# Layer 1 of a hybrid encoder: four pairs of projection tiles as quads of seven block products

## The chip, the cores and the metric

The kernel runs on one core of a Trainium2 chip. The metric is the device time of one execution in microseconds (us). Five engines with queues of their own work side by side: TensorE (PE, with its weight loads shown as PEld), VectorE (DVE), ScalarE (ACT), GpSimd (POOL) and SyncE (SP). On POOL and SP this kernel only issues transfers.

## The reference, cut to what matters

Two layers over 1024 positions of width 1024. Each layer begins with a norm and one wide projection:

```
hn = rmsnorm(h, norm1_g[layer])
proj = hn @ w_in[layer]                     # 1024 x 3328
u, q, k, v = proj[..., :512], proj[..., 512:1024], proj[..., 1024:1152], proj[..., 1152:1280]
gate_a, gate_b = sigmoid(proj[..., 1280:2304]), sigmoid(proj[..., 2304:])
y_a = s5_branch(u, ...)                     # two-way state-space scan, 32 groups, gelu, GLU
y_b = windowed_gqa(q, k, v, ...)            # 8 heads, blocks of 128 positions, window 128
merged = gate_a * (y_a @ w_branch_a) + gate_b * (y_b @ w_branch_b)
h = h + merged @ w_out;   h = h + swiglu_ffn(rmsnorm(h, norm2_g[layer]))
```

## The kernel before, in words

Activations lie transposed: 128 channels on the partitions, 1024 positions in two halves of 512 (h is 0 or 1). The 3328 columns of `w_in` are 26 tiles of 128: four of u, four of q (q0 to q3), one of k, one of v, eight of gate a (`ga`) and eight of gate b (`gb`). A half tile is one output of 128x512. Every fp32 operand is split into a high and a low part (`split`, `parts`), and a product of two operands takes three matmuls, so a half tile of a projection (`chain`, L175 to L177) is 8 blocks of 128 channels x 3 = 24 matmuls of 512 columns. Splitting the weights of a tile costs one cast on ACT (`whi`) and one subtraction on DVE (`wlo`), each 128x1024.

Work is a list of items, emitted in order (`emit`); the framework's scheduler then fixes the order of every engine's instructions when the program is compiled. Items that carry weights (`Granule`) also start loads of later weights. At most three plain weight tiles are split at a time. Activations lie in 86 slots of 128x512, and PSUM has 8 banks.

In layer 1 the items come in this order:

- The norm of both halves (`norm_parts`: `n0`, `n1`). The first half is normed while layer 0's last products run, the second between the first projections. PE works meanwhile on k, v and q0, first with half 0.
- q0, q1 and two half tiles of u.
- Attention (`attention_items`): 18 steps. Step i takes `round(per * (i + 1))` half tiles in all from the filler list (two more near the end), then computes the scores of unit i, the values of unit i - 2 and the transposes of unit i - 1. A unit is a key head group and a block of 128 queries. Here `per` is 1 and the list is two half tiles of u, then q2 and q3 (needed for the second key head), the rest of u and all gates: 42 half tiles. From step 12 on each step also starts one state scan (`s5_states`, q = 0 to 5).
- The S5 loop (`s5_items`): 9 iterations, again with filler, `per` 2. Iteration i has the output of state pair i (`s5_output`, PSUM tile `s5y`), and in i = 1 to 5 the states q = 2i + 4 and 2i + 5 (PSUM tile `s5x`, then on DVE L948 to L964, then four copies on ACT into `s5sg`, L968). The output of pair i needs the states 2i and 2i + 1, which the two iterations before have started. Between output and store lie a square on ACT, `s5w` on DVE (L997), a tanh on ACT (L998) and `s5g` on DVE (L1005).
- Four half tiles of filler around the loads of z, then the GLU, both branch products and `w_out`.

Layer 0 has the same attention and the same S5 loop, with 0.6 and 2.2 half tiles for `per`, and later in its loop half tiles of the branch product (`br`, 12 matmuls each) as filler.

The FFN already has a form that multiplies a pair of weight tiles against both halves of the positions as 2x2 blocks in the manner of Strassen and Winograd: seven block products in place of eight. A block product is 4 blocks of channels x 3 = 12 matmuls (`piece`, L186 to L188). `sums` forms sixteen combinations of the normed activations on DVE, `sum_pairs` splits them (`T`, 16 pairs, names `tt0` to `tt3`), `quad_part` forms the combinations of weights.

Of the kernel before, what the change touches and what calls it, by code (L numbers as in the profile page):

```python
# [8 lines left out]
F32 = mybir.dt.float32  # L9
# [4 lines left out]
ADD, SUB, MUL = ALU.add, ALU.subtract, ALU.mult  # L14
# [7 lines left out]
HC = 512  # L22
# [9 lines left out]
M_U, M_Q, M_K, M_V, M_GA, M_GB = 0, 4, 8, 9, 10, 18  # L32
# [63 lines left out]
class Trunk:  # L96
# [579 lines left out]
    def w_in(self, l, m):  # L676
        return Granule(self.t["w_in"][l, m].rearrange("p k c -> p (k c)"), DM)

    apart = None
# [185 lines left out]
    def attention_items(self, l, keys, q23, fill, per, tail):  # L865


        stage = {}
        fill = (list(fill[:2]) if l else []) + q23 + list(fill[2 if l else 0:])

        def scores(u):
            stage[u] = self.att_scores(l, u // 8, u % 8)

        def scale(u):
            self.att_scale(l, u // 8, *stage[u])

        def transpose(u):
            ex, k0, k1, _ = stage[u]
            stage[u] = (self.att_transpose(ex, k0, k1), k0, k1)

        def values(u):
            self.att_values(u // 8, u % 8, *stage.pop(u))

        taken = 0
        for i in range(18):
            want = min(len(fill), round(per * (i + 1)) + max(0, i - 15))
            self.add(fill[taken:want])
            taken = max(taken, want)
# [12 lines left out]
            self.add(tail.get(i, []))  # L901
            if i in (5, 7):
                self.add([keys[(i - 1) // 2]])
        return fill[taken:]

# [211 lines left out]
        return early, split, out  # L1117


    def w_out_items(self, l):  # L1120
        nc, V = self.nc, self.nc.vector
        self.h2 = {}
# [2 lines left out]
        src = self.t["xt"] if l == 0 else self.hs  # L1125
# [43 lines left out]
    def ffn_items(self, l, fill, head):  # L1169

        nc, V = self.nc, self.nc.vector
# [4 lines left out]
        early = quads < 4  # L1176
        ys = {} if early else None
# [48 lines left out]
        n0, n1 = (self.norm_parts(h, "rf", 2 * l + 1, lambda m, h=h: self.h2[m, h], lambda: self.hn2, ys) for h in range(2))  # L1226
        main = []
        blocks = []
        T = [[None] * 4 for _ in range(4)]

        def sums(j):

            at = ((j, 0), (j, 1), (j + 4, 0), (j + 4, 1))
            if early:
                y11, y12, y21, y22 = (ys.pop(a) for a in at)
            else:
                y11, y12, y21, y22 = (self.A("y") for _ in at)
                for y, (m, h) in zip((y11, y12, y21, y22), at):
                    hi, lo = self.hn2[h][m]
                    V.tensor_tensor(y, hi.bitcast(F32), lo.bitcast(F32), ADD)  # L1240
            V.tensor_tensor(y11, y12, y11, SUB)
            V.tensor_tensor(y12, y22, y12, SUB)
            V.tensor_tensor(y22, y22, y11, SUB)
            V.tensor_tensor(y21, y21, y22, SUB)
            for k, y in enumerate((y11, y22, y12, y21)):
                T[k][j] = (y, None)

        def sum_pairs(j, k):
            T[k][j] = self.split(T[k][j][0], f"tt{k}")

        def quad_items(f):

            q = Quad(self.t["w_gate"][l, f].rearrange("p k c -> p (k c)"), self.t["w_up"][l, f].rearrange("p k c -> p (k c)"))
            b = {}

            def product(bank, g, off, xs, start):
                def run():
                    if start:
                        b[bank] = self.PS(f"q{bank}")
                    self.piece(b[bank], g, off, xs(), start)  # L1260
                return (run, g)

            B = lambda h, a: lambda: self.hn2[h][a:a + 4]
            p = [product("x", q.a, 0, B(0, 0), True), product("y", q.b, HC, lambda: T[1], True),
                 product("v", q.b, 0, lambda: T[0], True), product("x", q.a, HC, B(0, 4), False),
                 product("y", q.c, 0, lambda: T[2], False), product("w", q.d, 0, lambda: T[3], True),
                 product("v", q.e, 0, B(1, 4), False)]

            def first():
                b["p1"] = self.A("qp")  # L1270
# [44 lines left out]
        made = {f: quad_items(f) for f in range(quads, NFF)}  # L1315
        orders = {}
        for gi, (f0, n) in enumerate(groups):
            for f in range(f0, f0 + n):
                if f in made:
                    p, e = made[f]  # L1320
# [29 lines left out]
            if f0 + n == quads:  # L1350
# [6 lines left out]
                w = 4 if early else 12  # L1357
# [4 lines left out]
        if fill:  # L1362
            a = len(head) + 12
            b = fill_end
# [4 lines left out]
    def build(self):  # L1369
        nc, V = self.nc, self.nc.vector  # L1370
# [30 lines left out]
        for l in range(DEPTH):  # L1401
# [23 lines left out]
            n0, n1 = (self.norm_parts(h, "ra", 2 * l, lambda m, h=h, src=src: src(m, h), lambda: self.hn) for h in range(2))  # L1425
            v1, v2 = self.halves(vc[0])
            loads, states = self.s5_head(l)
            tail_items = {11: pairs[:1] if l == 0 else []}
# [23 lines left out]
                self.add(pairs[1:])  # L1452
            else:

                k1, k2 = self.halves(kc[0])
# [174 lines left out]
```

## Time and profile before

| what | value |
|---|---|
| median of three runs | 2649.34 us (2649.23 to 2649.55) |
| the profiled execution | 2650.72 us, its span 2648.9 us |
| PE busy / DVE busy / ACT busy | 98% / 63% / 40% of the span |
| mean granted clock of TensorE | 0.993 |

The span runs from the first to the last instruction of the profiled execution; 1.8 us of its time lie outside. Busy shares are of the span; a matmul of 512 columns shows about 390 ns although the next one starts earlier, so a busy PE is read by the distance of starts.

### The profile page before, as it was taken

How to read it: one execution, taken by the hardware profiler on the slowest of the kernel's cores; microseconds unless marked ns; L12 is line 12 of the kernel's file. 1: busy time of each engine (PE TensorE's matmuls, PEld its weight loads, DVE VectorE, ACT ScalarE, POOL GpSimd, SP SyncE). 2: the span in 40 equal slices, each digit the busy share in tenths (PEclk: the TensorE clock that was granted, in tenths of full speed). 3: DMA queues.
4: the chain of work that ended last, by engine and by line, in shares of the span. 5: the costliest groups of instructions: out<-in, count | busy, mean ns of one | idle time of the engine just before them, and what ended most of it. 6: DMA issues, size and time to landing. Idle time of an engine off the chain costs nothing.

```text
span 2648.9 us, 35135 instructions
## 1 busy us (share of the span) xinstructions
PE 2590.7 (98%) x12878; PEld 2108.2 (80%) x12878; DVE 1659.1 (63%) x3333; ACT 1058.1 (40%) x2037; POOL 359.5 (14%) x524
## 2 busy tenths in 40 slices
PE   8999999999999999999999999999999999999997
PEld 6786677887788888888877778888878888888886
DVE  8985878575986745544673576646376545654556
ACT  5335743422443433333344553343235433333332
POOL 0141001000142220121010001100002220122010
PEclk9999999999999999999999999999999999999998
DMA  3453345354283652564342235434315652455253
GB/s 138 134 186 114 126 136 180 118 188 143 60 203 106 124 108 62 110 126 96 78 170 76 72 128 184 147 121 166 128 64 113 132 124 61 92 121 114 60 108 135
DMA packets 157438, 321.36 MB, mean 121 GB/s; under 512 B 20768, under 2 KB 55840, under 8 KB 157264
## 3 DMA queue, kind: packets, MB, share of 16 engines
q1 hardware_dynamic: 106192, 201.68, 23.1%
q0 software_dynamic: 51072, 117.43, 20.3%
q8 instruction: 101, 1.65, 0.3%
q14 instruction: 73, 0.60, 0.1%
HBM read 196.37 MB, written 122.63 MB: 120 GB/s over the span
## 4 chain that ended last, share of the span: by engine, by line
PE 89%; DVE 7%; DMA 2%; ACT 2%; issue 1%; SPq 0%; DVEq 0%; ACTq 0%
PE pj L175 6%; PE pj L176 6%; PE pj L177 6%; PE dn L175 6%; PE dn L176 6%; PE dn L177 6%; PE qy L186 2%; PE qx L186 2%; PE qv L186 2%; PE qv L188 2%; PE qy L188 2%; PE qx L188 2%; PE qv L187 2%; PE qx L187 2%; PE qy L187 2%; PE wo L175 2%
## 5 line engine op out<-in xcount | busy, mean ns | idle before, releaser
L164 DVE TENSOR_TENSOR wlo<-raw,whi 128x1024 fp32r<-128x1024 f32 (+3 forms) x210 | 186.3, 887 | 265.6 <-ACT whi L163 254.6
L163 ACT CAST whi<-raw 128x1024 fp32r<-128x1024 f32 (+3 forms) x210 | 163.8, 780 | 365.7 <-PE pj L176 118.0
L175 PE MATMUL pj<-rah,whi 128*128 128x512 f32 x768 | 306.1, 399 | 1.0 <-ACT rah L112 1.0
L176 PE MATMUL pj<-ral,whi 128*128 128x512 f32 x768 | 300.7, 392 | 1.3 <-DVE ral L113 1.3
L177 PE MATMUL pj<-rah,wlo 128*128 128x512 f32 x768 | 300.2, 391 | 0.0
L1208 POOL DMA_DIRECT2D hs<-dx x208 | 179.1, 869 | 845.0 <-ACT dx L1207 731.0
L175 PEld LDWEIGHTS pj<-rah,whi 128*128 128x128 f32 x768 | 145.0, 189 | 35.2 <-issue 3.3
L176 PEld LDWEIGHTS pj<-ral,whi 128*128 128x128 f32 x768 | 144.8, 189 | 31.4 <-DVE ral L113 3.2
L177 PEld LDWEIGHTS pj<-rah,wlo 128*128 128x128 f32 x768 | 144.8, 188 | 30.8
L1207 ACT COPY dx<-dn 128x512 f32<-128x512 f32 x208 | 121.2, 584 | 76.3 <-PE dn L177 75.6
L796 DVE CUSTOM_DVE_ANT_0 x<-s,bias,nsink 128x384 f32<-128x384 f32 (+1 forms) x128 | 67.6, 578 | 67.9 <-PE s L790 67.3
L186 PE MATMUL qx<-rfh,whi 128*128 128x512 f32 x280 | 108.9, 389 | 0.0
L187 PE MATMUL qx<-rfl,whi 128*128 128x512 f32 x280 | 108.9, 389 | 0.0
L188 PE MATMUL qx<-rfh,wlo 128*128 128x512 f32 x280 | 108.9, 389 | 0.0
L968 ACT COPY s5sg<-s5s 64x256 f32<-64x256 f32 x128 | 51.7, 404 | 132.8 <-DVE s5s L963 125.1
L175 PE MATMUL wo<-mgh,whi 128*128 128x512 f32 x256 | 100.0, 391 | 0.0
L177 PE MATMUL wo<-mgh,wlo 128*128 128x512 f32 x256 | 99.6, 389 | 0.0
L176 PE MATMUL wo<-mgl,whi 128*128 128x512 f32 x256 | 99.6, 389 | 0.0
L112 ACT CAST ffah<-ts 128x512 fp32r<-128x512 f32 x35 | 21.7, 621 | 191.2 <-DVE ts L1290 191.2
L175 PE MATMUL dn<-ffbh,whi 128*128 128x512 f32 x232 | 91.3, 394 | 0.0
L176 PE MATMUL dn<-ffbl,whi 128*128 128x512 f32 x232 | 90.6, 390 | 0.0
L176 PE MATMUL dn<-ffal,whi 128*128 128x512 f32 x232 | 90.4, 390 | 0.0
(430 smaller groups left out, 6695.7 us busy)
## 6 DMA issues: line engine op xcount, KB each, us to landing
hs<-dx POOLq DMA_DIRECT2D x208, 256.0 KB, 6.2
raw<-in_w_in SPq DMA_DIRECT2D x52, 512.0 KB
raw<-in_w_gate SPq DMA_DIRECT2D x44, 512.0 KB
raw<-in_w_up SPq DMA_DIRECT2D x44, 512.0 KB
raw<-in_w_down SPq DMA_DIRECT2D x96, 192.0 KB
g<-th POOLq DMA_DIRECT2D x64, 256.0 KB, 2.8
thr<-g SPq DMA_DIRECT2D x64, 256.0 KB
hs<-h POOLq DMA_DIRECT2D x48, 256.0 KB, 2.3
```

Source lines behind the costliest of these rows:

```text
L163: nc.scalar.copy(g.hi[:, :n], g.raw[:, :n])
L164: nc.vector.tensor_tensor(g.lo[:, :n], g.raw[:, :n], g.hi[:, :n].bitcast(F32), SUB)
L175: mm(ps, lhsT=wh, rhs=xh, start=k == 0, stop=False)
L176: mm(ps, lhsT=wh, rhs=xl, start=False, stop=False)
L177: mm(ps, lhsT=wl, rhs=xh, start=False, stop=k == n - 1)
L186: mm(ps, lhsT=wh, rhs=xh, start=start and k == 0, stop=False)
L187: mm(ps, lhsT=wh, rhs=xl, start=False, stop=False)
L188: mm(ps, lhsT=wl, rhs=xh, start=False, stop=k == len(xs) - 1)
L796: V.tensor_tensor_reduce(out=x[:, :n], in0=ps[:, :n], in1=self.bias[hd][:, bo:bo + n], op0=ADD, op1=ALU.min, scale=-1.0, scalar=self.nsink ...
L968: nc.scalar.copy(SG[64 * r:64 * r + 64, g * 256:(g + 1) * 256].rearrange("p (d n) -> p d n", d=2), Sv[64 * g:64 * g + 64, :, r])
L1207: nc.scalar.copy(t, ps)
L1208: nc.gpsimd.dma_start(self.hs[m, h], t, accum_op=ADD)
```

## The change

In layer 1 the eight tiles u0 to u3, k with v, and q0 with q1 become four quads. `tile_u`, `tile_kv` and `tile_q` are called with `grab` set, which collects their tile numbers and their closing functions; `linear_quads` then builds the seven products of each pair, sums the four results on DVE (five additions) and one copy on ACT, and hands each half tile to the closing function. The sixteen sums and their splits are formed once and serve all four quads. Three tiles of gate b, as plain products, take the place of k, v and q0 at the start of the layer. All four key tiles are made before attention. The filler list of attention and S5 loop is now q2, q3 and thirteen gate tiles (30 half tiles), and `per` falls from 1 to 0.9 and from 2 to 1. In numbers, with Python's rounding: steps 4 and 15 of attention get no filler, the other sixteen steps as many as before; in the S5 loop each iteration gets one half tile in place of two, and three in place of four are left behind the loop.

```diff
+        if self.grab is not None:
+            self.grab.append((m, done))
+            return []
...
-        fill = (list(fill[:2]) if l else []) + q23 + list(fill[2 if l else 0:])
+        fill = q23 + list(fill)
...
+    def quad_products(self, src1, src2, pairs, T):
+        q = Quad(*(s.rearrange("p k c -> p (k c)") for s in (src1, src2)))
...
+        return [product("x", q.a, 0, B(0, 0), True), product("y", q.b, HC, lambda: T[1], True),
+                product("v", q.b, 0, lambda: T[0], True), product("x", q.a, HC, B(0, 4), False),
+                product("y", q.c, 0, lambda: T[2], False), product("w", q.d, 0, lambda: T[3], True),
+                product("v", q.e, 0, B(1, 4), False)], b
...
+    def linear_quads(self, l, made, T):
...
+            def first(b=b):
+                b["p1"] = self.A("qp")
+                nc.scalar.copy(b["p1"], b["x"])
+            def second(b=b):
+                b["u2"] = self.A("qu")
+                V.tensor_tensor(b["u2"], b["p1"], b["y"], ADD)
+            def out11(b=b, done=done1):
+                done(0, b["x"])
+            def sum22(b=b):
+                V.tensor_tensor(b["p1"], b["p1"], b["y"], ADD)
+                b["c22"] = self.A("qc")
+                V.tensor_tensor(b["c22"], b["p1"], b["v"], ADD)
+            def out2(b=b, done=done2):
+                V.tensor_tensor(b["p1"], b["p1"], b["w"], ADD)
+                done(0, b["p1"])
+                done(1, b["c22"])
+            def out12(b=b, done=done1):
+                V.tensor_tensor(b["u2"], b["u2"], b["v"], ADD)
+                done(1, b["u2"])
...
+                us = self.linear_quads(l, [lambda i=i: self.tile_u(l, i) for i in range(4)], T)
+                kvq = self.linear_quads(l, [lambda: self.tile_kv(l, M_K, kn), lambda: self.tile_kv(l, M_V, vn),
+                                            lambda: self.tile_q(l, 0), lambda: self.tile_q(l, 1)], T)
+                a, c = (self.halves(x) for x in (gb[0], gb[2]))
...
-                         [k1, n1[0], k2, v1, n1[1], n1[2], v2, n1[3], n1[4], n1[5], qc[0], ke[0], ve[0], qe[0], kc[1], ke[1],
-                          vc[1], ve[1]] + keys[:2] + [qc[1], qe[1], vals, bias0] + q1 + us[:2])
-                left = self.attention_items(l, keys, q23, us[2:] + gb + ga, 1, tail_items)
+                         [a[0], n1[0], a[1], c[0], n1[1], n1[2], c[1], n1[3], n1[4], n1[5], gb[4], *s[:2], gb[1], *s[2:], *sp[1],
+                          gb[3], *sp[0], gb[5], *sp[2], *sp[3]] + us + kvq[:15] + keys + kvq[15:17] + [vals] + kvq[17:] + [bias0])
+                left = self.attention_items(l, [None] * 4, q23, gb[6:] + ga, 0.9, tail_items)
...
-                left = self.s5_items(l, left, 2)
+                left = self.s5_items(l, left, 1)
```

`sums` and `sum_pairs` move unchanged from `ffn_items` into functions of their own, and `gb[2m]`, `gb[2m + 1]` are the two half tiles of gate tile m.

## Rows read from the trace of the kernel before

**Rows 1.** The page: busy time, then its share in 40 slices.

```profile
PE 2590.7 (98%) x12878; PEld 2108.2 (80%) x12878; DVE 1659.1 (63%) x3333; ACT 1058.1 (40%) x2037; POOL 359.5 (14%) x524
PE   8999999999999999999999999999999999999997
```

**Rows 2.** Windows by stage, layer 1: stretch, length, busy PE, PEld, DVE, ACT, POOL.

```profile
1424.00:1539.00 115.00, 115.00 (x679) 85.75 (x678) 60.75 (x218) 64.97 (x175) 4.87 (x9) 1.00 0.25 83
1539.00:1602.80 63.80, 61.95 (x389) 46.69 (x388) 45.37 (x123) 30.16 (x72) 3.28 (x7) 1.00 0.30 100
...
1632.60:1696.90 64.30, 64.30 (x417) 53.58 (x416) 52.86 (x110) 25.77 (x53) 14.40 (x24) 1.00 0.54 180
...
1713.10:1756.70 43.60, 43.60 (x196) 36.10 (x194) 13.26 (x19) 15.86 (x27) 3.78 (x7) 1.00 0.45 151
```

**Rows 3.** Windows, three quads of layer 1's FFN, columns as before.

```profile
2024.86:2081.98 57.12, 57.12 (x252) 46.89 (x251) 32.33 (x52) 23.62 (x44) 12.09 (x14) 1.00 0.57 116
```

**Rows 4.** Timeline of PE, one attention step: start, duration, instruction.

```profile
1452.49 0.48 PE L175 MATMUL pj<-rah,whi 128*128 128x512 f32 x1
...
1458.14 1.58 PE L790 MATMUL s<-kk,qn 64*128 64x128 f32 x16
```

**Rows 5.** Timeline of DVE, one full iteration of layer 1's S5 loop.

```profile
1636.51 0.69 DVE L948 TENSOR_TENSOR s5a<-s5x,s5tb 128x512 f32<-128x512 f32 x1
...
1652.59 0.69 DVE L948 TENSOR_TENSOR s5a<-s5x,s5tb 128x512 f32<-128x512 f32 x1
```

**Rows 6.** Timeline of DVE, layer 0's S5 loop, iterations with little filler.

```profile
427.73 0.68 DVE L948 TENSOR_TENSOR s5a<-s5x,s5tb 128x512 f32<-128x512 f32 x1
...
433.13 0.68 DVE L948 TENSOR_TENSOR s5a<-s5x,s5tb 128x512 f32<-128x512 f32 x1
...
440.67 0.69 DVE L1005 SCALAR_TENSOR_TENSOR s5g<-s5g,s5y 128x512 f32<-128x512 f32 x1 [1.47 <-ACT s5g L998]
441.28 0.68 DVE L948 TENSOR_TENSOR s5a<-s5x,s5tb 128x512 f32<-128x512 f32 x1
...
457.16 0.68 DVE L948 TENSOR_TENSOR s5a<-s5x,s5tb 128x512 f32<-128x512 f32 x1
```

**Rows 7.** Timeline of PE, the same iterations of layer 0.

```profile
447.60 1.10 PE L940 MATMUL s5x<-s5uk,s5wbt 128*64 128x128 f32 x16
...
457.29 1.98 PE L940 MATMUL s5x<-s5uk,s5wbt 128*64 128x128 f32 x16 [5.66 <-DVE s5g L1005]
```

**Rows 8.** Windows, the end of that stretch; the first column behind POOL is the clock.

```profile
434.19:463.84 29.65, 23.99 (x161) 19.88 (x160) 25.08 (x54) 11.99 (x26) 4.73 (x8) 0.88 0.49 153
```

**Rows 9.** Waits of PE in layer 0's attention: total us, times, longest.

```profile
PE pv L836 <- DVE x L813: 1.4, 1, 1.4
PE pv L836 <- ACT p L823: 1.2, 2, 1.0
```

**Rows 10.** Timeline of DVE, the last scores of layer 1's attention.

```profile
1571.93 1.22 DVE L164 TENSOR_TENSOR wlo<-raw,whi 128x1024 fp32r<-128x1024 f32 x1
1573.06 0.48 DVE L796 CUSTOM_DVE_ANT_0 x<-s,bias,nsink 128x256 f32<-128x256 f32 x1
```

**Rows 11.** Timeline of PE, the same place.

```profile
1563.80 0.50 PE L175 MATMUL pj<-rah,whi 128*128 128x512 f32 x1
...
1573.60 0.66 PE L821 MATMUL pt<-cst,x 128*128 128x128 f32 x4 [0.54 <-DVE sm L796]
```

**Rows 12.** Timeline of PE, start of layer 1, directly behind the last norm matmuls.

```profile
1371.29 0.48 PE L175 MATMUL pj<-rah,whi 128*128 128x512 f32 x1
```

**Rows 13.** Timeline of DVE, start of layer 1, end of the second norm.

```profile
1381.29 1.46 DVE L113 TENSOR_TENSOR ral<-y,rah 128x512 fp32r<-128x512 f32 x2
1386.07 1.23 DVE L164 TENSOR_TENSOR wlo<-raw,whi 128x1024 fp32r<-128x1024 f32 x1 [3.32 <-ACT whi L163]
```

**Rows 14.** Timeline of DVE, two of the sixteen sums of layer 1's FFN.

```profile
1984.38 1.28 DVE L1241 TENSOR_TENSOR y<-y 128x512 f32<-128x512 f32 x2
```

**Rows 15.** Timeline of ACT, the copies behind one state.

```profile
454.20 1.67 ACT L968 COPY s5sg<-s5s 64x256 f32<-64x256 f32 x4 [4.54 <-DVE s5s L963]
```

More of the change, by code (lines that the diff above doesn't have):

```diff
@@ L677, in w_in @@
         return Granule(self.t["w_in"][l, m].rearrange("p k c -> p (k c)"), DM)
-    apart = None
+    apart = grab = None
     def proj(self, l, m, done, xs=None):
+        if self.grab is not None:
+            self.grab.append((m, done))
+            return []
         g = self.w_in(l, m)
@@ L901, in attention_items @@
             self.add(tail.get(i, []))
-            if i in (5, 7):
+            if i in (5, 7) and keys[-1]:
                 self.add([keys[(i - 1) // 2]])
@@ L1117, in glu_items, with sums @@
         return early, split, out
+    def sums(self, T, ys, pairs, j):
+        V = self.nc.vector
+        at = ((j, 0), (j, 1), (j + 4, 0), (j + 4, 1))
+        if ys is not None:
+            y11, y12, y21, y22 = (ys.pop(a) for a in at)
+        else:
+            y11, y12, y21, y22 = (self.A("y") for _ in at)
+            for y, (m, h) in zip((y11, y12, y21, y22), at):
+                hi, lo = pairs[h][m]
+                V.tensor_tensor(y, hi.bitcast(F32), lo.bitcast(F32), ADD)
+        V.tensor_tensor(y11, y12, y11, SUB)
+        V.tensor_tensor(y12, y22, y12, SUB)
+        V.tensor_tensor(y22, y22, y11, SUB)
+        V.tensor_tensor(y21, y21, y22, SUB)
+        for k, y in enumerate((y11, y22, y12, y21)):
+            T[k][j] = (y, None)
@@ new lines, in sum_pairs, with product, run @@
+    def sum_pairs(self, T, j, k):
+        T[k][j] = self.split(T[k][j][0], f"tt{k}")
+    def quad_products(self, src1, src2, pairs, T):
+        q = Quad(*(s.rearrange("p k c -> p (k c)") for s in (src1, src2)))
+        b = {}
+        def product(bank, g, off, xs, start):
+            def run():
+                if start:
+                    b[bank] = self.PS(f"q{bank}")
+                self.piece(b[bank], g, off, xs(), start)
+            return (run, g)
+        B = lambda h, a: lambda: pairs()[h][a:a + 4]
+        return [product("x", q.a, 0, B(0, 0), True), product("y", q.b, HC, lambda: T[1], True),
+                product("v", q.b, 0, lambda: T[0], True), product("x", q.a, HC, B(0, 4), False),
+                product("y", q.c, 0, lambda: T[2], False), product("w", q.d, 0, lambda: T[3], True),
+                product("v", q.e, 0, B(1, 4), False)], b
@@ new lines, in linear_quads @@
+    def linear_quads(self, l, made, T):
+        nc, V = self.nc, self.nc.vector
+        self.grab = tiles = []
+        for f in made:
+            f()
+        self.grab = None
+        out, nxt = [], []
+        for (m1, done1), (m2, done2) in zip(tiles[::2], tiles[1::2]):
+            p, b = self.quad_products(self.t["w_in"][l, m1], self.t["w_in"][l, m2], lambda: self.hn, T)
+            def first(b=b):
[17 more added lines that the diff above has]
+                done(1, b["u2"])
+            nxt.append((p, [(fn,) for fn in (first, second, out11, sum22, out2, out12)]))
+        for k, (p, e) in enumerate(nxt):
+            if k == 0:
+                out.append(p[0])
+            out += [p[1], e[0], p[2], e[1], p[3], p[4], e[2], p[5], e[3]]
+            if k + 1 < len(nxt):
+                out.append(nxt[k + 1][0][0])
+            out += [e[4], p[6], e[5]]
+        return out
@@ L1231, in sums @@
         def sums(j):
[L1233 to L1246, printed above, removed]
+            self.sums(T, ys, self.hn2, j)
         def sum_pairs(j, k):
-            T[k][j] = self.split(T[k][j][0], f"tt{k}")
+            self.sum_pairs(T, j, k)
         def quad_items(f):
[L1253 to L1267, printed above, removed]
+            p, b = self.quad_products(self.t["w_gate"][l, f], self.t["w_up"][l, f], lambda: self.hn2, T)
             def first():
@@ L1424, in build @@
             src = (lambda m, h: xs[h][m]) if l == 0 else (lambda m, h: self.h2[m, h])
-            n0, n1 = (self.norm_parts(h, "ra", 2 * l, lambda m, h=h, src=src: src(m, h), lambda: self.hn) for h in range(2))
+            ys, T = {}, [[None] * 4 for _ in range(4)]
+            n0, n1 = (self.norm_parts(h, "ra", 2 * l, lambda m, h=h, src=src: src(m, h), lambda: self.hn, ys if l else None)
+                      for h in range(2))
             v1, v2 = self.halves(vc[0])
@@ L1453, in build @@
             else:
[L1455 removed]
+                s = [(lambda j=j, T=T, ys=ys: self.sums(T, ys, self.hn, j),) for j in range(4)]
+                sp = [[(lambda j=j, k=k, T=T: self.sum_pairs(T, j, k),) for j in range(4)] for k in range(4)]
+                kn, vn = [], []
+                keys = [(lambda kn=kn, kv=kv, t=t: self.key_tiles(kn, kv, t),) for kv in range(2) for t in range(2)]
+                vals = (lambda vn=vn: self.value_tiles(vn),)
+                us = self.linear_quads(l, [lambda i=i: self.tile_u(l, i) for i in range(4)], T)
+                kvq = self.linear_quads(l, [lambda: self.tile_kv(l, M_K, kn), lambda: self.tile_kv(l, M_V, vn),
+                                            lambda: self.tile_q(l, 0), lambda: self.tile_q(l, 1)], T)
+                a, c = (self.halves(x) for x in (gb[0], gb[2]))
                 self.add(tail[:-6] + [n0[0]] + tail[-6:-4] + [n0[1], n0[2], tail[-4], n0[3], tail[-3], n0[4], tail[-2], n0[5],
                                                               tail[-1], (start_layer,)] +
[L1458 to L1460 removed]
+                         [a[0], n1[0], a[1], c[0], n1[1], n1[2], c[1], n1[3], n1[4], n1[5], gb[4], *s[:2], gb[1], *s[2:], *sp[1],
+                          gb[3], *sp[0], gb[5], *sp[2], *sp[3]] + us + kvq[:15] + keys + kvq[15:17] + [vals] + kvq[17:] + [bias0])
+                left = self.attention_items(l, [None] * 4, q23, gb[6:] + ga, 0.9, tail_items)
             def done_b(m, h, ps):
```

## The prediction

> **What bounds the kernel now.** I read the page first: PE is busy 98% of the span and at 9 tenths in nearly every slice, DVE 63% [rows 1]. So PE sets the end, and a matmul saved is time saved, but only where PE stays the last to be ready. A mean over the span can't tell that, so the windows by stage come next. In attention (1424 to 1539) DVE is busy 60.75 of 115.00 us. Where the first states join (1539 to 1602.8) it is 45.37 of 63.80, and PE already loses 1.85. In the S5 loop (1632.6 to 1696.9) it is 52.86 of 64.30, with PE full [rows 2]. The reader is to see that the filler keeps PE in front there: DVE has 82% of the loop's time, so the loop can't become much shorter however little PE has to do. The timelines give the two paces, and layer 0, whose loop has iterations with about half the filler, shows what comes of it.
>
> **The saving on PE.** Three quads are 252 matmuls in 57.12 us: 0.2267 each, with DVE busy 32.33 and ACT 23.62 of that time [rows 3]. A pair of plain tiles is 96 matmuls, a quad 84. Four quads save 48 x 0.2267 = 10.9 us. The Trainium skill ("TensorE: Matmul & The Clock Gate", Back-to-back issue gap) gives 215.7 ns for an isolated pair of matmuls of 512 columns and 131 ns for a sustained stream. By the second figure the saving would be an estimated 6.3 us; the trace of this case shows 0.2267 and decides.
>
> Twelve half tiles also leave attention and loop. Between transposes and scores one takes 1458.14 - 1452.49 = 5.65 [rows 4], in an unbroken run 24 x 0.2267 = 5.44. I count 12 x 0.18 = 2.1 saved (0 to 2.5). Together -13.0.
>
> The quads' own five additions and their splits lie beside 19 us of PE each, as in the FFN, whose quads have more additions and leave DVE idle 43% of the time [rows 3]: 0. Uncovered they would cost 5 x 0.6 = 3 each. The first filler of attention (5.65) covers the last quad's addition and the copies of q1: 0. The bias loads move behind the last quad on SP's queue; that same filler is their cover, and I take 0.
>
> **The start of layer 1.** Three gate tiles stand where k, v and q0 stood, so PE arrives as before up to the norm. But DVE now has the sums. It is free at 1381.29 + 1.2 = 1382.5 [rows 13]. Sixteen sums at 0.60 [rows 14] reach 1392.1; four subtractions for `tt1` 1394.5; the first quad's `wlo`, 1.1 [rows 13], 1395.6; four for `tt0` 1398.0; three additions for the second weight tile 1399.8; its cast and subtraction about 1401.5. PE goes on behind the last norm matmuls at 1371.29 [rows 12]; then come 12 matmuls, four half tiles and the first product: 1371.3 + 2.7 + 21.8 + 2.7 = 1398.5. The second product needs `tt1` and the second weight tile, and waits 3 us; queued behind it are all quads. The order may let the weights go first; 0 to 4, I take 2.
>
> **Step 4 of attention without filler.** Layer 0 has such steps: its waits of PE for scaled scores or copied transposes are 1.4 and 1.2 us in three cases [rows 9]. I take +1 (0 to 1.4).
>
> **Step 15 without filler.** Here DVE is behind. In the trace its minimum for the last scores begins at 1573.06, directly behind a `wlo` of 1.1 [rows 10], and the transposes wait for a bank which that minimum frees [rows 11]. The half tile that goes had begun at 1563.80 [rows 11] and only filled this time. PE comes 5.65 earlier to the same wait, which ends at most one `wlo` earlier: 5.65 - 1.1 = +4.5 (3 to 5.65).
>
> **The S5 loop.** Before, an iteration is 1652.59 - 1636.51 = 16.08 [rows 5], set by PE: two half tiles (11.3) and 4.8 for output and states. With one it would be 10.4. DVE can't follow. A state takes 433.13 - 427.73 = 5.40; two of them, `s5w`, the wait of 1.47 for the tanh and `s5g` make 441.28 - 427.73 = 13.55, and with a weight split among them 457.16 - 441.28 = 15.88 [rows 6]. There PE had two branch half tiles (24 matmuls) in an iteration, the amount that the change leaves, and it stood 5.66 us on DVE's `s5g` [rows 7]. No matmul behind a waiting one went ahead.
>
> Now for five such iterations. The last output needs state 15. From the start of state 6 that is four iterations, two states and the copies of 1.67 [rows 15]: 54.2 + 10.8 + 1.7 = 66.7, plus two weight splits at 1.1 to 2.3, about 70. PE has in the same time one half tile and a state issue (6.6), four iterations of 10.4 and an output with a half tile (8.4): 56.6. So PE idles 13 us. If DVE filled its waits for tanh and casts, four of 1.47 each and about 1 more, 6.5 would remain; with 15.88 for every iteration it would be 19. I take 13.
>
> After the wait of 5.66 the next sixteen `s5x` took 1.98 instead of 1.10 [rows 7], and the stretch had a granted clock of 0.88 [rows 8]: 0.12 x 29.65 / 0.5 = 7.1 us at the lower of the two levels, 1.2 GHz. Half of that, 3.6, is the most that can be lost, 0.9 the least; the part in which PE worked points to 2.6. Only the last gap counts in full, since before it PE has time: +2.6.
>
> Behind the loop 43.6 us of half tiles covered the way of z to the GLU [rows 2]; five are left, 27 us. I see nothing in the chain (two DVE steps, two on ACT, a store and a load) that fills this: 0.
>
> **Sum.** -13.0 + 2 + 1 + 4.5 + 13 + 2.6 = +10.1 us. On the profiled execution's 2650.72 (span 2648.9) that is 2660.8; the median of the runs is 1.4 lower, so 2659.4. The bounds of the terms taken alone give -3 to +21.
>
> **Rivals.** The measurement tells about 0.2% (5.3 us) from no change.
>
> *The saving arrives whole.* DVE never idles in the loop and is ahead when it begins, and nothing in attention waits. Then -13 + 2: 2638. For it speaks 98% PE [rows 1]; against it layer 0, where PE stood on DVE. The Trainium skill ("Perfetto Trace Analysis", Identifying the Most-Contended Engine) says to improve the engine with the highest occupancy first. By that rule PE's saving is the time's, the 2638 just given; layer 0's wait shows a stage where it isn't. 10%.
>
> *Half tiles go ahead of stalled outputs.* The compiled order may put later half tiles of the loop before an output that it sees late. DVE's chain stays, but the five half tiles behind the loop can move into it; about 19 us of idle time go, the clock's share too, and the GLU comes when z does: 2641. Against it: layer 0's order kept its half tiles in place. It decides against my sign once more than 5 us of the idle time are filled. 12%.
>
> *DVE's waits are filled, half tiles stay.* Loop at 6.5, no clock loss: -13 + 2 + 1 + 4.5 + 6.5 = +1: 2650. It needs states ready to run while a tanh is out, which PE, ahead by then, could provide; in layer 0 it didn't happen. 22%.
>
> *Loads come late too.* With shorter iterations a state's tables have less time. At 2 us in five iterations: 2669. 6%.
>
> **How the numbers follow.** My forecast holds 50%, its own range 2655 to 2666. Slower by over 0.2%: 0.50 + 0.06 = 0.56. Within: 0.22. Faster: 0.10 + 0.12 = 0.22. The range from 2639 to 2667 leaves out the first and the last rival, 16%.
>
> **What would show it.** Right: in the loop, DVE's states follow each other at 5.40 without a wait for `s5x`, iterations are 13.5 to 16 us apart, and PE's waits before `s5y` name `s5sg` (or `s5x` waits for `s5g`), some 13 us in all; the clock dips near the last; at the end of attention PE waits for DVE about 4 us; the first quad's `qy` waits 2 or 3. The four quads take 19.04 each. Wrong: a loop of about 10.4 us an iteration with PE full, DVE not behind; or waits inside the quads, for slots or for DVE, which I priced at nothing; or a wait before the GLU.

## The result, and the profile after

The changed kernel takes 2668.9 us (2666.8 to 2673.1, 6 runs) beside 2650.6 of the kernel before (2649.2 to 2659.6, 6 runs): a ratio of 1.007 (95%: 1.006 to 1.0079). It is slower, as forecast, but by 18 us and not by 10: the time lies 1.9 us above the range. The profiled execution took 2666.78 us, 16.1 more than that of before.

The page of the profile, its span and busy line, and the row of PE and that of DVE in 40 slices, answer to [rows 1]:

```profile
span 2665.0 us, 35170 instructions
PE 2588.0 (97%) x12830; PEld 2105.8 (79%) x12830; DVE 1708.2 (64%) x3413; ACT 1077.6 (40%) x2069; POOL 360.2 (14%) x524
PE   8999999999999999999989999899999999999997
DVE  8976878565986745554686457866466545554556
```

PE has 48 matmuls less and is busy only 2.7 us less; the span has grown by 16.1. So some 19 us are new idle time, and part of the saved work has come back as slower work. The waits of PE in layer 1 (1330 to 1790 us; in total, times, longest) say where it stands idle:

```profile
PE s5x L943 <- DMA s5uk<-ud: 10.3, 2, 5.6
PE qw L186 <- ACT whs L151: 4.6, 1, 4.6
PE s5x L943 <- issue: 3.0, 1, 3.0
PE qx L186 <- ACT qp L1175: 1.1, 1, 1.1
PE pv L839 <- ACT p L826: 0.4, 1, 0.4
PE pt L824 <- ACT th L770: 0.3, 1, 0.3
```

The windows of the changed kernel (PE, PEld, DVE, ACT and POOL busy, then the granted clock) around these waits: the norm stretch, the first quad, the end of attention, the S5 loop, and the way from its last output to the GLU. They answer to [rows 2]:

```profile
1356.80:1372.34 15.54, 13.71 (x53) 10.82 (x52) 9.75 (x25) 3.95 (x7) 1.64 (x3) 0.78 0.14 52
1396.90:1420.50 23.60, 19.01 (x73) 15.10 (x72) 21.63 (x33) 14.16 (x24) 1.64 (x3) 0.86 0.30 96
1618.00:1650.00 32.00, 28.30 (x183) 21.09 (x180) 24.42 (x71) 16.19 (x42) 1.63 (x3) 0.95 0.37 124
1659.68:1742.26 82.58, 72.27 (x498) 61.64 (x497) 69.66 (x149) 29.79 (x63) 16.10 (x27) 0.94 0.60 192
1742.26:1772.15 29.89, 29.89 (x145) 25.20 (x144) 13.71 (x21) 15.85 (x29) 5.19 (x9) 1.00 0.54 171
```

The reader is to see two things. Each of the four windows with a wait has a granted clock below 1.00. And the last window is full: nothing waits ahead of the GLU.

The first quad on PE's timeline (start, duration, engine, line, operation):

```profile
1404.87 0.39 PE L188 MATMUL qv<-tt0h,wlo 128*128 128x512 f32 x1
1409.85 0.80 PE L186 MATMUL qw<-tt3h,whs 128*128 128x512 f32 x1 [4.59 <-ACT whs L151]
1410.44 0.68 PE L186 MATMUL qx<-rah,whi 128*128 128x512 f32 x1
1410.92 0.63 PE L187 MATMUL qx<-ral,whi 128*128 128x512 f32 x1
1411.35 0.63 PE L188 MATMUL qx<-rah,wlo 128*128 128x512 f32 x1
```

`qx`, `qy` and `qv` came without a wait, the forecast wait of `qy` among them. But the order has one matmul of `qw` ahead of the second `qx` product, which could have run, and `qw` needs `tt3` and the fourth weight part, among the last things that DVE and ACT make. DVE is back to back here (21.63 of 23.60). On ACT this row of casts ends the wait:

```profile
1405.11 1.05 ACT L151 CAST whi<-sm 128x1024 fp32r<-128x1024 f32 x1 [0.57 <-PE qv L187]
1406.06 1.14 ACT L112 CAST tt2h<-y 128x512 fp32r<-128x512 f32 x2
1407.10 2.18 ACT L112 CAST tt3h<-y 128x512 fp32r<-128x512 f32 x4
1409.18 0.62 ACT L151 CAST whs<-raw 128x512 fp32r<-128x512 f32 x1
```

The first of them waits for PE's `qv` product; then ACT casts without a pause until 1409.80, and the part for `qw` comes last. Behind the wait matmuls start 0.43 apart instead of 0.23: the lower of the two clock levels. That `qx` product takes 4.87 us instead of 2.72. From the end of the norm to the first scores the stage takes 116.1 us. The other three quads take 2.72 a product with no wait but the 1.1.

At step 15 of attention, a row of DVE and one of PE:

```profile
1629.11 0.28 DVE L846 COPY yb<-pv 128x128 f32<-128x128 f32 x1
1629.49 1.56 PE L943 MATMUL s5x<-s5uk,s5wbt 128*64 128x128 f32 x16 [2.98 <-issue]
```

The transposes go through without a wait, and the state's `s5x` behind them stands 2.98 us. The profile names no releaser; the wait ends 0.1 us after DVE's copy `yb`, which had stood behind the steps of the state before.

In the S5 loop PE's two waits and DVE at the same time:

```profile
1687.97 1.97 PE L943 MATMUL s5x<-s5uk,s5wbt 128*64 128x128 f32 x16 [5.60 <-DMA s5uk<-ud]
1689.87 0.80 PE L175 MATMUL pj<-rah,whi 128*128 128x512 f32 x1
1715.33 1.98 PE L943 MATMUL s5x<-s5uk,s5wbt 128*64 128x128 f32 x16 [4.71 <-DMA s5uk<-ud]
```

```profile
1687.62 0.68 DVE L951 TENSOR_TENSOR s5a<-s5x,s5tb 128x512 f32<-128x512 f32 x1
1693.02 0.68 DVE L951 TENSOR_TENSOR s5a<-s5x,s5tb 128x512 f32<-128x512 f32 x1
1698.42 0.68 DVE L1000 SCALAR_TENSOR_TENSOR s5w<-s5g,s5y 128x512 f32<-128x512 f32 x1
1700.57 0.69 DVE L1008 SCALAR_TENSOR_TENSOR s5g<-s5g,s5y 128x512 f32<-128x512 f32 x1 [1.47 <-ACT s5g L1001]
1701.17 0.68 DVE L951 TENSOR_TENSOR s5a<-s5x,s5tb 128x512 f32<-128x512 f32 x1
```

DVE goes from state to state at 5.40, with an iteration of 13.55, as in layer 0 [rows 6]; it waits for `s5x` once, 1.9 us at the loop's first state, and not again. Yet PE's waits name a load. SyncE's queue in the loop (waits, then timeline) shows why:

```profile
SPq L124 <- DVE wlo L164: 50.2, 4, 16.9
```

```profile
1679.59 0.34 SPq L124 DMA_DIRECT2D raw<-in_w_glu  x1
1679.97 0.43 SPq L918 DMA_DIRECT2D s5wbt<-sp  x1
1681.39 0.43 SPq L923 DMA_DIRECT2D s5uk<-ud  x1
```

A weight load waits for DVE's `wlo` to free its buffer, and the loads of the states' tables are queued behind it. PE's fourth `s5x` of the loop needs the fourth of these loads. Its `s5uk` is issued at 1681.39, with 512 KB of weights and three tables of 256 KB ahead of it since 1679.59, and PE waits for it until 1687.97, while DVE is still at the state before. So DVE's chain and the loads may each hold the loop.

### The profile page after: what moved, and what is told of

Read it like the earlier page. It is cut to its first block, busy times and chain, and to the rows that moved or that the text cites. A ratio compares the mean times of both kernels' runs of the same rounds, so it can differ in the third digit from the quotient of the medians.

```text
span 2665.0 us, 35170 instructions
## 1 busy us (share of the span) xinstructions
PE 2588.0 (97%) x12830; PEld 2105.8 (79%) x12830; DVE 1708.2 (64%) x3413; ACT 1077.6 (40%) x2069; POOL 360.2 (14%) x524
## 4 chain that ended last, share of the span: by engine, by line
PE 86%; DVE 6%; DMA 2%; issue 2%; ACT 2%; POOL 1%; SPq 0%; DVEq 0%; ACTq 0%; POOLq 0%
PE dn L175 6%; PE dn L176 6%; PE dn L177 6%; PE pj L175 4%; PE pj L176 4%; PE pj L177 4%; PE qx L186 3%; PE qx L187 3%; PE qx L188 3%; PE qy L186 3%; PE qy L187 3%; PE qv L187 3%; PE qv L186 3%; PE qy L188 3%; PE qv L188 3%; PE wo L175 2%
## 5 line engine op out<-in xcount | busy, mean ns | idle before, releaser
L164 DVE TENSOR_TENSOR wlo<-raw,whi 128x1024 fp32r<-128x1024 f32 (+3 forms) x202 | 176.7, 875 | 211.0 <-ACT whi L163 203.8
L163 ACT CAST whi<-raw 128x1024 fp32r<-128x1024 f32 (+3 forms) x202 | 155.7, 771 | 328.6 <-PE pj L176 82.7
L175 PE MATMUL pj<-rah,whi 128*128 128x512 f32 x640 | 257.6, 403 | 1.1 <-ACT rah L112 1.0
L176 PE MATMUL pj<-ral,whi 128*128 128x512 f32 x640 | 252.4, 395 | 1.3 <-DVE ral L113 1.3
L177 PE MATMUL pj<-rah,wlo 128*128 128x512 f32 x640 | 251.5, 393 | 0.0
L175 PEld LDWEIGHTS pj<-rah,whi 128*128 128x128 f32 x640 | 122.0, 191 | 30.3 <-issue 4.0
L176 PEld LDWEIGHTS pj<-ral,whi 128*128 128x128 f32 x640 | 121.9, 191 | 26.9 <-DVE ral L113 3.2
L177 PEld LDWEIGHTS pj<-rah,wlo 128*128 128x128 f32 x640 | 121.7, 190 | 26.0
L772 POOL DMA_DIRECT2D g<-th x64 | 36.0, 562 | 411.6 <-ACT th L770 411.5
```

Of the source, the lines that this page charges most:

```text
L163: nc.scalar.copy(g.hi[:, :n], g.raw[:, :n])
L164: nc.vector.tensor_tensor(g.lo[:, :n], g.raw[:, :n], g.hi[:, :n].bitcast(F32), SUB)
L175: mm(ps, lhsT=wh, rhs=xh, start=k == 0, stop=False)
L176: mm(ps, lhsT=wh, rhs=xl, start=False, stop=False)
L177: mm(ps, lhsT=wl, rhs=xh, start=False, stop=k == n - 1)
```

## The experiments

Medians of the kernel before lay between 2649.7 and 2651.0 us in these comparisons. Times are medians, with the ratio to before and its interval where it matters.

**Filler from attention into the loop.**

```diff
-left = self.attention_items(l, [None] * 4, q23, gb[6:] + ga, 0.9, tail_items)
+left = self.attention_items(l, [None] * 4, q23, gb[6:] + ga, 0.6, tail_items)
-left = self.s5_items(l, left, 1)
+left = self.s5_items(l, left, 1.6)
```

> Six half tiles less in attention (13 instead of 19), eight more in the S5 loop (14 instead of 6), fewer behind it. The changed kernel's quads stay as they are. Theory 1 (VectorE's chain of states paces the loop and PE has too little beside it): the loop from the first s5y to the last gets longer by the half tiles put in (about 8 x 5.6 = 45 us), but its idle time of 10.3 us before s5x and about 3 us of low clock go; attention without half tiles costs 1 to 2 us at its own steps. Time 2668.9 - 12 = about 2657 (2653 to 2661). Theory 2 (the loads of the states' tables, late behind a weight load on SP's queue, pace the loop): longer iterations give the loads more time too, so also a gain, but with weight loads added among them; 2657 to 2664. Theory 3 (the loss is the phase of the clock, not the order of work): no change beyond 4 us.

(Counted by the code, five half tiles move: attention has 13 instead of 18, the loop 14 instead of 9, and three stay behind it in both.) Measured 2665.9 us (1.0058, 1.0043 to 1.0073). The loop's waits fall from 10.3 to 4.6, and attention's grow from 3.7 to 7.3. Both theories that forecast a gain miss, and the time, 3.0 below the change, is within what theory 3 allows. But the waits moved with the filler, so the order of work matters: attention has no filler to give.

**Loads earlier.**

```diff
-        return ([(lambda q=q: load(q),) for q in range(n)],
+        return ([(lambda q=q: load(q),) for q in range(n + 2 * l)],
...
-                self.item(lambda q=2 * j + 2: load(q))
+                self.item(lambda q=2 * j + 2 + 2 * l: load(q))
...
```

> Layer 1's table loads of states are issued one iteration earlier (two more before the loop, each later one two states ahead of its old place). Theory 1 (VectorE's chain paces the loop): VectorE never waited for a table, so 0 (within 2 us), and the two waits of s5x stay at 5.6 and 4.7 us. Theory 2 (late loads pace it): the two waits named with the tables' loads go, time about 10 us less, 2659.

Measured 2672.3 us (1.0081, 1.0066 to 1.0096). That is theory 1's time, or a little more, but not its waits: those for loads are gone, and this row of PE's waits in the loop has come in their place:

```profile
PE s5y L987 <- ACT s5sg L971: 7.0, 3, 4.1
```

With four more at the GLU, whose cover has fallen from 29.89 to 18.62 us because two half tiles now run inside the loop, the idle time is what it was. VectorE's chain holds the loop alone as well.

**The store behind the next state.**

```diff
-            if end:
+            if end and not (l and on):
                 self.item(lambda i=o - 1: self.s5_store(i, st))
...
+            if end and l and on:
+                self.item(lambda i=o - 1: self.s5_store(i, st))
```

> In layer 1's loop the store step (s5g, which waits 1.47 us for the tanh) comes behind the first of the next two states instead of ahead of it, so VectorE has work while the tanh is out. Theory 1 (VectorE's chain paces the loop): five waits of 1.47 = 7 us leave VectorE's loop, PE's idle time falls by as much: 2662 (2660 to 2664). Theory 2 (late loads pace it): 0, since the states come no earlier than their tables; 2669.

Measured 2669.9 us (1.0072, 1.0055 to 1.0089). It says nothing about either theory: the framework's scheduler left the order on PE, DVE and ACT as it was, and DVE kept its five waits for the tanh in the loop (6.5 us). It serves as a second trace of the change: loop 84.7 us instead of 82.6. So a loop's length is known to about 2 us from one trace.

**No sums.**

```diff
-        V.tensor_tensor(y11, y12, y11, SUB)
...
+        if not plain:
+            V.tensor_tensor(y11, y12, y11, SUB)
...
```

> Leaves out part of the computation: the sixteen subtractions that make the sums of the block products in layer 1's first four quads (the operands are the plain normed values instead), 16 x 0.6 = 9.6 us of VectorE ahead of the first quad. Theory 1 (VectorE's backlog at the start of layer 1 costs the first quad's wait of 4.6 us and the low clock behind it): that wait and the 2.2 us of slow matmuls go, 2669 - 7 = 2662 (2660 to 2664). Rival (the first quad waits for ScalarE's own queue of casts, not for VectorE's sums): the wait stays, 0 to -2.

Measured 2670.0 us (1.0069, 1.0054 to 1.0085). The wait at `qw` fell from 4.6 to 2.5 and the stage by 2.9 us, which the time of a run doesn't show. The sums are about half of that wait. For the rest ACT's cast `whi` waits 3.0 us for PE's `qv` here, and two casts of `tt3` and the part for `qw` stand behind it. Both expectations miss.

**Lighter states.**

```diff
+        if l and q >= 6:
+            Sv = zv
+        else:
             S, b2 = self.A("s5s"), self.A("s5c")
...
```

> Leaves out part of the computation: in layer 1 the states 6 to 15 skip their last four VectorE steps (the rotation back), and ScalarE copies the scanned values instead. That takes about 2.0 us of VectorE from each of ten states, 20 us from the loop. Theory 1 (VectorE's chain of states paces the loop, and each wait of PE costs a stretch of low clock on top): the waits of s5x (10.3 us) and the clock loss in the loop (about 5 us by the windows) go: 2668.9 - 15 = 2654 (2651 to 2658). Theory 2 (loads pace it): the waits named with the tables stay, within 2 us of 2669.

Measured 2665.4 us (1.0065, 1.005 to 1.008), and the loop 81.6 us, where the two traces of the change have 82.6 and 84.7. With 19 us less work VectorE now stands idle, and PE still waits for loads:

```profile
1702.67 0.69 DVE L951 TENSOR_TENSOR s5a<-s5x,s5tb 128x512 f32<-128x512 f32 x1 [4.25 <-PE s5x L943]
```

```profile
1717.25 1.98 PE L943 MATMUL s5x<-s5uk,s5wbt 128*64 128x128 f32 x16 [4.04 <-DMA s5uk<-ud]
```

VectorE alone, theory 1 as first stated, falls. Two iterations take 27.3 us here (10.48 and 16.82), paced by the loads, beside 28.2 in the changed kernel (13.55 and 14.70 on DVE): two limits lie 1 us apart, by these two traces.

**Both: early loads and lighter states** (the two edits together).

> Leaves out part of the computation, as before: layer 1's states 6 to 15 skip their last four VectorE steps. With it, layer 1's table loads are issued one iteration earlier. Each of the two alone moved the time by less than 4 us. Theory A (two limits of the loop lie side by side, VectorE's chain at about 28 us and the loads behind a weight load at about 27 us per two iterations, so that either alone still holds it): with both gone the loop's waits of 10.3 us and its clock loss go: 2668.9 - 13 = 2656 (2652 to 2660). Theory B (a third limit, PSUM banks or ScalarE's copies): waits of 7 us or more stay, 2665 to 2671.

Measured 2655.9 us (1.002, 1.0011 to 1.003). The loop has no wait left; its window:

```profile
1662.47:1731.13 68.66, 68.66 (x498) 59.13 (x497) 50.42 (x111) 31.73 (x67) 16.79 (x29) 1.00 0.66 215
```

82.58 - 68.66 = 13.9 us is what loop idling cost, 10.3 of it waits and 3.6 low clock (16.1 beside the second trace of the change). Of the two theories it is A.

**Cover at the start.**

```diff
-gb[3], *sp[0], gb[5], *sp[2], *sp[3]] + us + ...
+gb[3], *sp[0], gb[5], *sp[2], gb[6], *sp[3], gb[7]] + us + ...
-left = self.attention_items(l, [None] * 4, q23, gb[6:] + ga, 0.9, tail_items)
+left = self.attention_items(l, [None] * 4, q23, gb[8:] + ga, 0.8, tail_items)
```

> Two more plain half tiles (11 us of PE) stand before the first quad; attention gives them up (16 half tiles instead of 18), the loop keeps 9 and 3 stay behind it. Theory 1 (VectorE's and ScalarE's backlog of sums and splits at the first quad): the waits of 4.6 and 1.1 us and the clock loss behind them (about 3.5) go, less 1 to 2 us for new waits in attention: 2668.9 - 7 = 2662 (2659 to 2665). Rival (the first quad waits for its own second weight tile, not for the backlog): the wait stays, 2668 to 2671.

Measured 2661.4 us (1.0048, 1.0033 to 1.0063), 7.5 less than the change, as theory 1 said. All of PE's waits from the norm to the last state of attention:

```profile
PE pv L839 <- ACT p L826: 1.8, 2, 1.6
PE qx L186 <- ACT qp L1175: 1.1, 1, 1.1
PE pt L824 <- ACT th L770: 0.5, 1, 0.5
PE s5x L943 <- ACT th L770: 0.5, 1, 0.5
```

The wait of 4.6 has gone, and so has the one of 3.0 at step 15, which now has filler. From the end of the norm to the first scores it takes 119.7 us, with 48 matmuls more than the change: 119.7 - 48 x 0.2267 = 108.8, so the wait at `qw` and the low clock behind it cost 116.1 - 108.8 = 7.3. In this run's order no matmul of `qw` stands ahead of the second `qx` product either. Cover and order have changed together, and no run parts them.

**States earlier.**

```diff
-        n = 2 * S5_LEAD
+        n = 2 * (S5_LEAD + 2 * l)
...
```

> Layer 1 starts its states four steps earlier: ten of the sixteen in attention (from step 8 on) and six in the loop, instead of six and ten; filler as in the changed kernel. Theory 1 (VectorE's work is bunched in the loop while it has room in attention): loop without waits, about 10 us of idle time and 5 us of clock less, and 1 to 3 us of new waits at the end of attention: 2668.9 - 13 = 2656 (2652 to 2661). Theory 2 (loads queued behind weight loads on SP's queue pace the states): the loads stand as close to their states as before, so the wait moves into attention: 2666 to 2671.

Measured 2668.4 us (1.007, 1.0053 to 1.0086). A miss for theory 1: attention and loop together take 255.1 us instead of 253.8. The time is in theory 2's range, but not as that theory said: one wait for loads (5.1) stays in the loop, and attention's waits, which grew from 3.7 to 8.3, name no load.

**Holes of known size in the kernel before.** The first run has nine copies in a place where DVE could do them early:

```diff
+                def hold(n):
+                    for k in range(n + 1):
+                        t = self.hn[k == n][0][0]
+                        V.tensor_copy(t, t.bitcast(F32))
```

> The kernel before, with nine in-place copies on VectorE (128x512, of one normed tile, exact) set between two projections at the start of layer 1, where TensorE's next matmuls must wait for them. The price of a hole by itself: TensorE stands 3 to 6 us. If a hole costs its own length: 2649.7 + 3 to 6. If a hole of this length brings a stretch of low clock behind it, as the windows of the changed kernel show behind each of its holes (1.7 to 3.5 us lost): 2649.7 + 6 to 9.5, with a granted clock below 1.00 in the 50 us behind the hole.

Measured 2649.1 us (0.9998, 0.9988 to 1.0007): the copies ran beside PE, and no hole came about. But this trace, in the order of before, has the slow norm stretch of the changed kernel, 15.55 us instead of 12.39 (this run, then the kernel before):

```profile
1359.58:1375.13 15.55, 13.72 (x53) 10.74 (x52) 9.72 (x25) 3.32 (x6) 1.09 (x2) 0.78 0.09 35
1358.90:1371.29 12.39, 10.56 (x53) 8.22 (x52) 9.74 (x25) 3.35 (x6) 1.09 (x2) 1.00 0.12 44
```

The run with earlier loads, with the changed kernel's order up to there, has the short one, 12.37. So that stretch's 3.1 us come and go with the execution; the change didn't make them. The next two runs copy the last tile that PE reads:

```diff
+                def hold():
+                    t = self.hn[1][7][0]
+                    for k in range(8):
+                        V.tensor_copy(t, t.bitcast(F32))
+                    for h in range(2):
+                        x = self.hn[h][0][0]
+                        V.scalar_tensor_tensor(x, t.bitcast(F32), 0.0, x.bitcast(F32), MUL, ADD)
```

> The kernel before with a hole of known place: eight in-place copies of the last tile that the projections of q0 read, then one exact step each on the two tiles that q1 begins with, all on VectorE, so that TensorE stands 4 to 6 us at the start of layer 1. If a hole costs its own length, 2650 + 4 to 6 = 2654 to 2656. If a hole of this length brings a stretch of low clock behind it (1.7 to 3.5 us): 2656 to 2660, with a granted clock below 1.00 in the 50 us behind the hole.

> As the hole of eight copies, but with two: TensorE stands 1.5 to 2.5 us. If every hole brings a stretch of low clock: 2650 + 3 to 6. If a hole this short brings none (the waits of 1 us in the kernel before left the granted clock at 1.00): 2650 + 1.5 to 2.5, clock 1.00 behind it.

Eight copies: 2656.6 us (1.0023, 1.0014 to 1.0032); two: 2652.0 us (1.0007, 0.9998 to 1.0016). The first matmul and the third behind each hole, then the window from the hole to the scores, of the kernel with eight and of that with two:

```profile
1399.36 0.50 PE L175 MATMUL pj<-rah,whi 128*128 128x512 f32 x1 [4.67 <-DVE rah L1461]
1400.01 0.63 PE L177 MATMUL pj<-rah,wlo 128*128 128x512 f32 x1
```

```profile
1399.36:1428.37 29.01, 29.01 (x120) 23.58 (x120) 2.99 (x3) 5.38 (x8) 1.08 (x2) 0.94 0.16 54
```

```profile
1401.22 0.50 PE L175 MATMUL pj<-rah,whi 128*128 128x512 f32 x1 [1.90 <-DVE rah L1461]
1401.80 0.39 PE L177 MATMUL pj<-rah,wlo 128*128 128x512 f32 x1
```

```profile
1401.22:1428.65 27.43, 27.43 (x121) 22.45 (x121) 3.00 (x3) 5.39 (x9) 1.08 (x2) 1.00 0.23 77
```

The stage from the projections to the scores, 52.80 us before, takes 59.31 with the hole of 4.67 and 54.96 with that of 1.90. The long hole costs 6.5, its length and 1.8 at the lower clock (29.01 x 0.06 = 1.7); the short one 2.2, with the clock at 1.00. The Trainium skill ("TensorE: Matmul & The Clock Gate", HAM oscillation) says that behind a wait that is long enough the next burst of matmuls starts at the lower clock. The traces agree in kind: the clock fell behind the wait of 4.67 us and stayed at 1.00 behind that of 1.90.

**Branch products in the loop.** On top of the cover at the start:

```diff
-            tail_items = {11: pairs[:1] if l == 0 else []}
+            tail_items = {11: pairs[:1]}
...
-                left = self.s5_items(l, left, 1)
+                self.add(pairs[1:])
+                left = self.s5_items(l, self.mix(left[:9], bb[:8]), 1.9) + left[9:]
```

> A version that may beat both: two more half tiles of cover before the first quad (as in the experiment on cover at the start, 2661.4), and eight half tiles of the attention branch product (12 matmuls each, 21.8 us) moved from behind the GLU into the S5 loop, with the splits of the attention output done before the loop. If the loop is held by VectorE and loads at about 28 us per two iterations and PE only lacks work there, its 11.3 us of waits and the low clock behind them go: 2661.4 - 14 = 2647 (2643 to 2652). If the added weight splits and weight loads lengthen the loop by as much as they fill: 2655 to 2662.

Measured 2659.3 us (1.0041, 1.0028 to 1.0054). Waits for loads keep 8.0 us in the loop, and the splits of the attention output put 3.6 into attention. With early loads as well:

> Cover at the start, eight branch half tiles in the loop, and layer 1's table loads one iteration earlier. If the loads behind the weight loads hold the last iterations of the version with branch products (waits of 8.0 us there, iterations of 18.9 and 14.5 against 13.4), these waits and about 1.5 us of clock go: 2659.3 - 9 = 2650 (2647 to 2653). If VectorE's chain with its added weight splits holds them, the waits move to the outputs: 2656 to 2660.

Measured 2654.8 us (1.0018, 1.0009 to 1.0026). That lies between the two forecasts: the loop's waits fall to 1.1, and attention's 3.6, 1.9 and 1.8 stay. Without the branch products, cover and early loads alone:

> Cover at the start and early loads, filler as in the experiment on cover. If VectorE's chain holds the loop as soon as the loads don't (as the waits of 7.0 us for the states' copies said when loads alone were moved): 2661.4 - 2 = 2659 (2657 to 2663). If the loads were the only limit: 2661.4 - 15 = 2647.

Measured 2662.4 us (1.0046, 1.0033 to 1.0059): the waits for `s5sg` of 7.0 are back. While the whole computation stands, early loads alone gain nothing; with branch products as work for PE they did. More gates in the loop, with branch products as cover of the GLU (`per` 1.25, and `bb[:6]` behind the attention output's splits):

> Cover at the start, early loads, eleven gate half tiles in the loop instead of nine, and six branch half tiles in place of two gates as cover for the GLU behind the loop. If TensorE only lacks work beside VectorE's chain in the loop: about 7 us of waits go and the GLU has its cover: 2659 - 8 = 2651 (2647 to 2655). If the added weight splits lengthen VectorE's chain by as much: 2657 to 2662.

Measured 2664.5 us (1.0053, 1.0039 to 1.0066). A miss: the loop waits 4.6, but the branch products now stand behind the splits:

```profile
PE br L175 <- ACT ybh L860: 6.4, 3, 5.7
```

**A version that beats both.** Cover, early loads, branch products, and the first splits of the attention output two steps earlier; the second run also shifts filler:

```diff
-            tail_items = {11: pairs[:1]}
+            tail_items = {9: pairs[:1]}
```

> As the version with cover, early loads and eight branch half tiles (2654.8), but the splits of the first half of the attention output come at step 9 of attention, beside filler, instead of step 11, ahead of the step without. If that wait of 3.6 us and its 1.5 us of low clock come from the splits standing ahead of the scores on VectorE: 2654.8 - 5 = 2650 (2648 to 2652). If only their place moves: 2653 to 2656.

Measured 2647.7 us (0.999, 0.9981 to 0.9999): the wait of 3.6 has gone.

```diff
-left = self.attention_items(l, [None] * 4, q23, gb[8:] + ga, 0.8, tail_items)
+left = self.attention_items(l, [None] * 4, q23, gb[8:] + ga, 0.85, tail_items)
-left = self.s5_items(l, self.mix(left[:9], bb[:8]), 1.9) + left[9:]
+left = self.s5_items(l, self.mix(left[:8], bb[:10]), 2.0) + left[8:]
```

> As the run with the splits at step 9, with one half tile more in attention and eight gates with ten branch half tiles in the loop. If attention's waits come from steps without filler: 1 to 3 us less than that run, 2648. If the loop's third weight split for branch products holds VectorE: 2651 to 2656.

Measured 2643.5 us (0.9975, 0.9966 to 0.9984), 25 us below the change and 6.6 below the kernel before, more than was expected. No run sets the same moves in the kernel before; there PE waits only 1.9 us from the end of the norm to the GLU, so they have little to gain. Its windows from the norm to the first scores, to the first output and to the last:

```profile
1375.29:1494.97 119.68, 118.56 (x528) 97.53 (x526) 74.16 (x106) 58.12 (x94) 8.15 (x15) 1.00 0.27 93
1494.97:1657.65 162.68, 160.47 (x993) 119.13 (x993) 108.79 (x348) 93.48 (x245) 7.06 (x13) 1.00 0.30 99
1657.65:1750.44 92.79, 92.41 (x604) 77.50 (x603) 76.03 (x156) 39.70 (x80) 14.99 (x25) 1.00 0.49 158
```

PE idles 3.7 us in 375, and the clock stays at 1.00. DVE is as busy in this loop (82%) as in the one before.

## Why the prediction was right in its sign and short in its size

- **The saving on PE, -13.0.** Nearly right, as a remainder. From the end of the norm to the GLU the run with early loads and lighter states takes 385.8 us and the kernel before 385.4. Off the first go 9.4 us of waits, 2.7 of low clock at the first quad (7.3 - 4.6) and 1.6 at the end of attention (0.05 x 32), off the second 1.9 of waits: 372.1 against 383.5, so 11.4 saved. The rate behind it is seen directly: three quads at 2.72 a product.
- **The start of layer 1, +2 (0 to 4). This is the step that failed.** It cost 8.4: the 7.3 worked out above and the wait of 1.1 for `qp`. The working followed DVE's queue to the operands of the second product, which came in time, and stopped there; the splits that came after were taken as covered, at nothing. It left out that ACT has a row of casts of its own for the sixteen splits, six of them still to do at 1406.06, that the fourth weight part is made behind them at 1409.18, and that the compiled order lets a matmul which needs both stand ahead of one that doesn't. And it priced the clock for the loop alone. The prediction had named waits inside the quads as a sign that it was wrong, and they came.
- **Step 4, +1.** No wait came: 0. **Step 15, +4.5.** 3.0 and 0.4 of waits and 1.6 of clock make 5.0: right in size, and DVE was behind as said. But the transposes, where the wait was forecast, had none. It came at `s5x`, and it ended before DVE's minimum of the last scores began at 1629.97, so it isn't the forecast wait for a bank. A wait of 0.3 is left at step 14. The 1.9 us that PE waited in attention before went away, which the sum didn't take off.
- **The S5 loop, +13, with clock +2.6.** Right in size, 13.9. The pace of DVE was as worked out: states at 5.40, iterations of 13.55 to 14.70, no half tile ahead of a stalled output, 69.5 us from the start of state 6 to the end of state 15, with its copies about 71, instead of about 70. But the releaser was another than forecast: PE's waits name the tables, and none names `s5sg` or `s5g`. The rival by which loads come late too was held to add its price to DVE's; the runs show it as a second limit beside DVE's. That its figure, 2669, is the measured one is luck: the loop cost no more than forecast, and the excess arose at the start. From the first output to the GLU either gained 3 us or less when relieved alone (1.0 for VectorE, 2.6 for the loads, about the spread of two traces); both together gave 13.9.
- **GLU cover, 0.** Right: 29.89 us of full PE.
- **Not in the sum:** the norm stretch at the lower clock, +3.1, which a trace in the order of before has too. In this pair of traces -11.4 + 8.4 + 0.3 + 5.0 + 13.9 - 1.9 + 3.1 makes 17.4; 2.1 less ahead of layer 1 and 0.7 more behind the GLU give 16.0 of the 16.1. The sum closes because the 11.4 is a remainder of the same stretches; it isn't a test of the terms. The medians stand 2 us further apart than the profiled executions. No stage accounts for that, and it stays open.

The forecast missed the profiled execution by 6.0 us, and the 6.4 that the start cost above its term are as much alone. The Trainium skill ("Perfetto Trace Analysis", Identifying the Most-Contended Engine) says to optimize the engine with the highest occupancy first. The prediction weighed a reading of it by which PE's saving is the time's. PE was the busiest in every trace here; the time rose by 18 us when 48 of its matmuls went, and fell by 25 with the same matmuls, through earlier loads and through work set where PE had waited.

## What to carry to other kernels

Work taken from the busiest engine is time only where that engine is not already the cover of another chain: before taking it away, read from a stage with less of it what the other engine's pace is, and look at the queue of the loads at that pace too, since two limits a microsecond apart made either cure look useless here. Follow the operands of a new start through every engine to the last one, not to the first that is late. And when a kernel gets lighter, move its filler: here the same saving went from +18 us to -6.6.

## What the runs showed of the hardware that was not expected

A hole of 4.67 us on TensorE cost 6.5, one of 1.90 cost 2.2; a wait in the loop of 5.6 us left the next sixteen `s5x` at 1.97 instead of 1.10 and the first matmuls behind them up to 0.59 and then 0.43 apart. The norm stretch, with waits of about 1.0 and 0.8 us in it, ran at a granted clock of 1.00 in some traces and of 0.78 in others, of both orders, and was 12.4 or 15.5 us long.
